# One run of 32 small products or two of 16: where the token sums stand among the dense products of a PEER layer

## The chip, the cores and the metric

One core of a Trainium2 chip runs the whole step as one program. The metric is the device time of one execution in microseconds (us); the time before is the median of three executions. Engines are named as in the profile: PE (matrix products) with its weight loads PEld, DVE, ACT, POOL (GpSimd) and SP, which only issues transfers here.

## The reference

A decoder layer on 576 tokens (512 of a prompt, 64 samples) of width 2048: a modulated norm, a projection, two recurrent branches, an output projection, then a PEER layer and a final norm. The change stands in the PEER layer, cut here to what matters:

```
q   = (h2 @ w_q)                          # 8 heads, two halves of 128
sc  = q . sub_keys                        # 128 first keys, 128 second keys
i1, i2, top = best 16 pairs of each head  # expert = i1 * 128 + i2, 16384 experts
act = gelu(h2 . expert_u[expert]) * softmax(top)
out = sum over heads and picks of act * expert_v[expert]
```

Each token picks 8 x 16 = 128 experts. Expert `(i1, i2)` is one row of 2048 numbers in `u` and one in `v`.

## The kernel before

Experts are kept in 128 blocks, one block for each first key. For the 512 prompt tokens the kernel computes the 80 most picked blocks (`L = 80`) densely, as matrix products over all tokens; picks outside of these, and all picks of the samples, are gathered row by row with indirect DMAs.

**The dense first half (U).** The loop `for n in range(NU2)` has 160 steps, two for each of the 80 blocks. `u_half` does a step: 8 values of `kk`, and at each three products of 128x128 weights with 128x512 numbers (high and low parts of a split, `hhi`, `hlo`, `xhi`, `xlo`), 24 products in all, into one bank `pu`. Even `n` has `k` = 0 to 7, odd `n` has `k` = 8 to 15; then GELU on ACT and a store. The weights of a step come by SP (`raw`), ACT copies out the high part `xhi` and POOL subtracts for the low part `xlo`, two to three steps ahead.

**The token sums.** The dense products need, for each token, how much it weighs each of the experts: a matrix of 128 second keys by 80 blocks. For each token, DVE makes two one-hot matrices of its 128 picks (`op` and `wr`, eight tokens at a time, `g_pair`, L1587), ACT scales one by the softmax (`g_scale`, L1595), and PE multiplies them (`g_mm`, L1601): four products of 32 columns side by side for each token. A block of four tokens fills a bank of PSUM by 16 such products, and ACT copies the bank to a staging tile `stg` (`g_out`, L1608), which is stored to `gd` and read again in the second half. There are 128 blocks, done two at a time: one into the bank `gbank`, one into the bank that `pu` does not use at that time (`other_bank`, tile `gx`). The next block of experts starts in that bank.

**What sets the order.** All engines work their instructions in the order in which the Python code writes them. A planner (`spare`, `upto`, `due_g`) decides in which step a pair of token blocks, a gathered row or a piece of the selection stands. Gathered rows of `u` are fetched by POOL (indirect DMA, `take`, L1234) and multiplied by DVE (L1262).

Of the kernel before, what the change touches and what calls it, by code (L numbers as in the profile page):

```python
# [51 lines left out]
LAG = 3  # L52
# [28 lines left out]
def build(ctx, tc, A, O, dbg=None):  # L81
# [292 lines left out]
    for n in ("lru_wa", "lru_wx"):  # L374
        g = wk.tile([128, KW, 64], F32, name=f"g_{n}")
# [261 lines left out]
    def pbank(tag, nm, bufs):  # L637

        if tag == "u":
            u_turn[0] += 1  # L640
            tag, bufs = f"u{u_turn[0] % 2}", 1
        return psum["p"].tile([128, 512], F32, name=nm, tag=tag, bufs=bufs)

    def other_bank(nm):

        return psum["p"].tile([128, 512], F32, name=nm, tag=f"u{(u_turn[0] + 1) % 2}", bufs=1)
# [196 lines left out]
    def new_row(nm):  # L843
        s_ = free_slot()
        if s_ is None:
            s_ = min(range(slots_now[0]), key=lambda x: held_by[x])
        k = held_by[s_] = len(row_log)
        row_log.append(False)
        return (gp if s_ < RB else pools["vx"]).tile([128, D], F32, name=nm, tag=f"row{s_}", bufs=1), k
# [4 lines left out]
    for i in range(RB):  # L854
        r, k = new_row(f"row0_{i}")
# [75 lines left out]
    def ahead(l, c):  # L931
        while at["l"] <= min(l, len(stream) - 1):
            load(at["l"])
            at["l"] += 1
        while at["c"] <= min(c, len(stream) - 1):
            conv(at["c"])
            at["c"] += 1
# [119 lines left out]
    def sample_twice():  # L1057

        for k0 in range(0, KD, 8):
            r, a = new_row(f"dup{k0}")  # L1060
            row_log[a] = True
            d = r.bitcast(F32R).rearrange("p (q k t) -> p q k t", q=2, t=128)
            dups.append(d)
            for q in range(2):
                S.activation(d[:, q].rearrange("p k (r t) -> p k r t", t=NG),
                             r32(hv[q][:, k0:k0 + 8, None, NA:T]).to_broadcast([128, 8, 2, NG]), AF.Copy)

    def sample_rows():

        hT = first_h["h"] = psum["p"].tile([128, D], F32, name="hT0", tag="hT", bufs=1)  # L1070
        for k in range(KD):
            for q in range(2):
                PE.matmul(hT[:, k * 128:(k + 1) * 128], dups[k // 8][:, q, k % 8, :], identr, start=q == 0, stop=q == 1)
# [310 lines left out]
    def mid(n):  # L1384
        for f in mids.pop(n, ()):
            f()
        if R1 is not None and gk and n % 2 == 0:
            g_eight(n)

    def u_half(n, i, c):  # L1390
        hi, lo = parts.pop(n)
        if c == 0:
            fin["pu"] = pbank("u", f"pu{i}", 2)
        pu = fin["pu"]
        for kk in range(8):
            k = 8 * c + kk
            if kk == 4:
                mid(n)
            for a, (st, mv) in enumerate(((hi, 0), (hi, 1), (lo, 0))):
                PE.matmul(pu, st[:, kk, :], movA[mv](k), start=k == 0 and a == 0, stop=k == KD - 1 and a == 2)  # L1400
        if c == 1:
            act = actp.tile([128, NA], F32, name=f"act{i}", tag="act")
            S.activation(act, pu, AF.Gelu_apprx_tanh)
            if i < L - SG:
                nc.scalar.dma_start(actd[i // SG, :, i % SG, :], act)
            else:
                kept.append(act)
# [161 lines left out]
    gk = {}  # L1569
# [21 lines left out]
    def g_scale(b):  # L1591

        ops, wr, j0 = pair[b]
        for j in range(4):
            S.activation(ops[:, j0 + j, :], ops[:, j0 + j, :], AF.Copy, scale=it[2][:, b * 4 + j:b * 4 + j + 1])  # L1595

    def g_mm(b, pg):
        ops, wr, j0 = pair.pop(b)
        for j in range(4):
            for a in range(0, 128, 32):  # L1600
                PE.matmul(pg[a:a + 32, j * L:(j + 1) * L], ops[:, j0 + j, a:a + 32], wr[:, j0 + j, :],  # L1601
                          start=True, stop=True)

    def g_out(b, pg):
        c, b0 = divmod(b, TC // 4)
        if b0 == 0:
            stg[c] = pools["rg"].tile([128, L, TC], F32, name=f"stg{c}", tag="stg", bufs=2)
        S.activation(stg[c][:, :, b0 * 4:b0 * 4 + 4].rearrange("p i t -> p t i"),  # L1608
                     pg[:, :4 * L].rearrange("p (t i) -> p t i", t=4), AF.Copy)
        if b0 == TC // 4 - 1:  # L1610
            full = stg.pop(c)
            for q in range(0, L, L // 4):
                puts.append(lambda q=q: nc.scalar.dma_start(gd[c][:, q:q + L // 4, :], full[:, q:q + L // 4, :]))

    def put(n):
        for f in puts[:n]:
            f()
        del puts[:n]
# [5 lines left out]
    spare, due_g = -BEHIND, 0.0  # L1624
    R1 = R2 = None
    gm = [0, 0, 0, 0, 0]
    ep = None

    def upto(n):
        return min(NB2, max(0, (n - R1) * NB2 // (E0 - 6 - R1)))  # L1630

    def g_eight(n):

        nonlocal spare
        b = gm[1]
        if b + 2 <= min(upto(n - LAG), gm[2]):
            pgs = gk["g"], other_bank(f"gx{b}")
            for j in range(2):
                g_mm(b + j, pgs[j])
            for j in range(2):  # L1640
                g_out(b + j, pgs[j])
            gm[1] += 2
            spare += 0.8

    for n in range(NU2):
        _, i, c = stream[n]
        if n == 0:
            sample_twice()
        if n == 1:
            sample_rows()  # L1650
        ahead(n + 3, n + 2)
        spare += PIECE if R1 is None else PIECE_G
        scaled = gm[2]
        if R1 is not None:
            put(2)
            if n % 2 and gk:
                g_eight(n)
            if not gk:
                g_start()
            elif gm[0] < min(upto(n), gm[1] + PAIRS - 1):  # L1660
                g_pair(gm[0])
                gm[0] += 2
                spare -= 2.2
            while n > R1 + 5 and gm[2] < min(gm[4], scaled + 4):
                g_scale(gm[2])
                gm[2] += 1
            gm[3:] = gm[0], gm[3]

        even, waits = R2 is not None, False
        while spare > 0 and R2 is None:  # L1670
            cost = next(steps1 if R1 is None else steps2, "end")
            if cost == "end":
                if R1 is None:
                    R1 = n
                else:
                    R2 = n
                break
            if cost is None:
                waits = True
                break  # L1680
            spare -= cost
        if not even:
            if since is None and ready[0]:
                since = n
            if since is not None and n == since + 1:
                fetch_to(RB - 1)
            if R1 is not None and n > R1 + 1 and gf[0] in h_fetch and gf[0] <= gu[0] + 2:
                fetch_to(gf[0] + 1)
            if since is not None and n > since + 2:
                due_g += RATE[R1 is not None] + (0.7 if waits and spare > 4.5 else 0.0)  # L1690
            g0 = gu[0]
            gather_to(due_g, ready[0])
            due_g = min(due_g, gu[0] + 1.0)
            spare -= 2.4 * (gu[0] - g0)
            if waits:
                spare = min(spare, 3.0)
            G0 = gu[0]
        else:
            gather_to(G0 + (NU + EARLY_V - G0) * (n - R2 - (1 - EASE) * max(0, n - E0)) / (EASE * (NU2 - 1) + (1 - EASE) * E0 - R2))
        if n == E0:  # L1700
            assert not pair and not stg
            put(len(puts))
            p2.close()
            epx = ctx.enter_context(ExitStack())
            ep = epx.enter_context(tc.tile_pool(name="ep", bufs=1))
        u_half(n, i, c)
        if n - E0 == 2:
            load_group(0)
        for sg, o in ((0, 1), (1, 7)):
            if 0 <= n - E0 - o < 4:  # L1710
                load_weights(sg, n - E0 - o)
        if n - E0 == 6:
            weigh(0)
        if n - E0 == 7:
            halve(0, 0)
        if n - E0 == 8:
            halve(0, 1)
        if n == NU2 - 2:
            weigh_kept(0)
            weigh_kept(1)  # L1720
        if n == NU2 - 1:
            weigh_kept(2)
# [38 lines left out]
    for i in VO:  # L1761
        c = GT[i][2]
# [3 lines left out]
    for m in range(M):  # L1766
        gi, q, bl, first, final = steps[m]
        n = NU2 + 2 * m
# [12 lines left out]
        for kq in range(KD // VQ):  # L1781
# [9 lines left out]
            k, pv = v_column(n, gi, q, bl, first, final, kq)  # L1791
# [34 lines left out]
    with tc.If(any_ > 0), tc.tile_pool(name="fb", bufs=1) as fp:  # L1826
        io1 = fp.tile([128, 128], F32, name="f_io1")
        V.tensor_scalar(io1, iota, 1.0, None, op0=ALU.add)
        for i, (p0, n, c) in enumerate(GT):
# [8 lines left out]
            kk = pick_keys(R_, f"f{i}", fp, io1, kb)  # L1838
# [117 lines left out]
```

## Time and profile before

| | |
|---|---|
| median of 3 executions | 3203.68 us (3203.2 to 3206.89) |
| the profiled execution | 3219.74 us, its span 3217.9 us |
| PE busy, share of the span | 3038.3 us, 94% |
| PE share of the chain that ended last | 74% |
| granted TensorE clock, mean | 0.978 |
| stretch of the token sums, from the span's start | 1526.7 to 2121 us |

PE's time in the profile is modelled and its products overlap: a 128x512 product is shown with some 390 ns, yet products start some 230 ns apart. So what PE costs is read from the starts of its instructions, not from their durations. In the profile each of the small products stands as two (the 16 of a token block as x32), since they multiply plain fp32 numbers. "Issue" as a reason for idle time means that the profile shows nothing that the engine waited for.

### The profile page before, as it was taken

To read this page: it belongs to the slowest core of one execution; us is meant where nothing else is said; L and a number is where in the kernel's file an instruction comes from. 1 tells how busy PE (TensorE), PEld (TensorE's weight loads), DVE (VectorE), ACT (ScalarE), POOL (GpSimd) and SP (SyncE) were. 2 spreads that over 40 slices of the span, in tenths; PEclk is the share of its full clock that TensorE was granted. 3 is DMA by queue.
4 is the path that set the end of the run, shared out by engine and by line. 5 is a ranking of instruction groups with operands and counts; after the bars stand their busy time and mean duration, and the time that the engine had idled before them with its cause. 6 is when DMAs were issued, how large, how long until landed. Compare 5 with 4: busy or idle time off the path is not lost.

```text
span 3217.9 us, 52757 instructions
## 1 busy us (share of the span) xinstructions
PE 3038.3 (94%) x20313; PEld 2568.9 (80%) x20313; DVE 2242.0 (70%) x3296; ACT 1042.8 (32%) x1645; POOL 1793.7 (56%) x1093
## 2 busy tenths in 40 slices
PE   5899999999989999999999999998999999889897
PEld 2688798899979898887887777787878778677776
DVE  5355521234356797988999988867787898888955
ACT  3244311123232223232655555532322222122222
POOL 2233233344333335666666666667877788777842
PEclk8999999999989999999999999999999999999998
DMA  9834465633332226999879998999999997999963
GB/s 364 308 132 139 159 215 203 213 111 117 130 134 101 73 74 216 314 326 373 339 300 378 365 398 324 371 389 362 367 403 401 400 358 286 372 372 371 352 207 138
DMA packets 257650, 881.13 MB, mean 274 GB/s; under 512 B 37190, under 2 KB 38086, under 8 KB 203494
## 3 DMA queue, kind: packets, MB, share of 16 engines
q0 software_dynamic: 75472, 454.32, 36.1%
q1 hardware_dynamic: 161760, 382.48, 33.7%
q10 hardware_dynamic: 20160, 40.90, 3.3%
q8 instruction: 160, 2.62, 0.3%
q14 instruction: 98, 0.80, 0.1%
HBM read 878.84 MB, written 65.76 MB: 294 GB/s over the span
## 4 chain that ended last, share of the span: by engine, by line
PE 74%; DMA 11%; DVE 7%; issue 4%; POOL 2%; ACT 1%; SPq 0%; POOLq 0%; ACTq 0%; DVEq 0%
PE pu L1400 25%; PE pv L1423 15%; PE pp_o L139 6%; DMA v<-v,rows 5%; PE pp_s L139 3%; PE pp_c L139 3%; PE pp_x L139 3%; PE pp_b L139 3%; PE qb L139 3%; PE pp_y L139 2%; PE qa L139 2%; PE ada L189 2%; DMA wa<-w_ada 2%; DMA raw<-vq 2%; DVE accB L1290 2%
## 5 line engine op out<-in xcount | busy, mean ns | idle before, releaser
L926 POOL TENSOR_TENSOR xlo<-raw,xhi 128x1024 fp32r<-128x1024 f32 x320 | 783.5, 2460 | 365.6 <-ACT xhi L925 359.4
L1262 DVE SCALAR_TENSOR_TENSOR u<-u,hT 128x2048 f32<-128x2048 f32 x223 | 504.8, 2283 | 126.9 <-DMA u<-u,rows 124.9
L1290 DVE SCALAR_TENSOR_TENSOR accB<-v,dots,accB 128x2048 f32<-128x2048 f32 x211 | 496.5, 2353 | 133.5 <-DMA v<-v,rows 128.8
L925 ACT ACTIVATE xhi<-raw 128x1024 fp32r<-128x1024 f32 x320 | 338.4, 1062 | 749.3 <-PE pv L1423 251.8
L1423 PE MATMUL pv<-ahi,xhi 128*128 128x512 f32 x1280 | 509.3, 398 | 49.6 <-DVE acc L1445 40.7
L1400 PE MATMUL pu<-hhi,xhi 128*128 128x512 f32 x1280 | 507.1, 396 | 1.0 <-ACT qt L949 0.7
L1423 PE MATMUL pv<-alo,xhi 128*128 128x512 f32 x1280 | 505.3, 395 | 2.3 <-DVE alo L1374 2.3
L1423 PE MATMUL pv<-ahi,xlo 128*128 128x512 f32 x1280 | 504.5, 394 | 1.2 <-POOL xlo L926 1.2
L1400 PE MATMUL pu<-hhi,xlo 128*128 128x512 f32 x1280 | 498.6, 390 | 2.3 <-POOL xlo L926 2.3
L1400 PE MATMUL pu<-hlo,xhi 128*128 128x512 f32 x1280 | 498.9, 390 | 0.0
L1423 PEld LDWEIGHTS pv<-ahi,xhi 128*128 128x128 f32 x1280 | 244.5, 191 | 109.4 <-DVE acc L1445 27.6
L1234 POOL DMA_INDIRECT v<-v,rows x223 | 265.7, 1191 | 78.9 <-issue 40.6
L1234 POOL DMA_INDIRECT u<-u,rows x223 | 225.1, 1009 | 116.1 <-DVE u L1262 68.0
L1400 PEld LDWEIGHTS pu<-hhi,xhi 128*128 128x128 f32 x1280 | 240.3, 188 | 58.8 <-issue 1.7
L1423 PEld LDWEIGHTS pv<-ahi,xlo 128*128 128x128 f32 x1280 | 244.4, 191 | 53.5 <-POOL xlo L926 1.6
L1423 PEld LDWEIGHTS pv<-alo,xhi 128*128 128x128 f32 x1280 | 244.7, 191 | 52.6 <-DVE alo L1374 2.6
L1400 PEld LDWEIGHTS pu<-hhi,xlo 128*128 128x128 f32 x1280 | 240.4, 188 | 54.3 <-POOL xlo L926 3.6
L1400 PEld LDWEIGHTS pu<-hlo,xhi 128*128 128x128 f32 x1280 | 240.6, 188 | 47.4
L1595 ACT ACTIVATE op<-op,it 128x128 f32<-128x128 f32 x512 | 155.9, 389 | 1.2 <-issue 0.8
L128 POOL TENSOR_TENSOR wlo_q<-raw_q,whi_q 128x1024 fp32r<-128x1024 f32 x28 | 68.2, 2438 | 149.0 <-ACT whi_q L126 145.8
L189 PE MATMUL ada<-wa,cpad 128*32 128x512 f32 x768 | 106.5, 650 | 43.2 <-DMA wa<-w_ada 43.0
L128 POOL TENSOR_TENSOR wlo_o<-raw_o,whi_o 128x1024 fp32r<-128x1024 f32 x32 | 77.6, 2426 | 115.9 <-ACT whi_o L126 115.9
(505 smaller groups left out, 5655.9 us busy)
## 6 DMA issues: line engine op xcount, KB each, us to landing
wa<-w_ada SPq DMA_DIRECT2D x96, 1024.0 KB
raw<-ut SPq DMA_DIRECT2D x160, 512.0 KB
raw<-vq SPq DMA_DIRECT2D x320, 256.0 KB
gd<-stg ACTq DMA_DIRECT2D x64, 320.0 KB
gsb<-gd POOLq DMA_DIRECT2D x80, 256.0 KB
actd<-act ACTq DMA_DIRECT2D x76, 256.0 KB
actr<-actd POOLq DMA_DIRECT2D x19, 1024.0 KB
raw_o<-w_out SPq DMA_DIRECT2D x32, 512.0 KB
```

Of the source, the lines that this page charges most:

```text
L128: lo_engine(share).tensor_sub(lo, raw, r32(hi))
L139: PE.matmul(o, st, mv[pick](k), start=first, stop=last)
L189: PE.matmul(acc[32 * g:32 * g + 32, :], cpad[:, 4 * kq + g, :], w[:, g, :], start=kq == 0, stop=kq == 3)
L925: S.activation(hi, raw, AF.Copy)
L926: G.tensor_sub(lo, raw, r32(hi))
L1234: G.indirect_dma_start(out=out, out_offset=None, in_=src, in_offset=bass.IndirectOffsetOnAxis(ap=idx, axis=0), bounds_check=NE * 128 - 1, ...
L1262: V.scalar_tensor_tensor(r, r, 1.0, st["h"], op0=ALU.mult, op1=ALU.mult, accum_out=dots[i][:, j:j + 1])
L1290: V.scalar_tensor_tensor(st["a"], r, dots[i][:, j:j + 1], st["a"], op0=ALU.mult, op1=ALU.add)
L1400: PE.matmul(pu, st[:, kk, :], movA[mv](k), start=k == 0 and a == 0, stop=k == KD - 1 and a == 2)
L1423: PE.matmul(pv, st, mv, start=first and j == 0 and a == 0, stop=last and not end and j == SG - 1 and a == 2)
L1595: S.activation(ops[:, j0 + j, :], ops[:, j0 + j, :], AF.Copy, scale=it[2][:, b * 4 + j:b * 4 + j + 1])
```

## The change

`g_eight` did the two token blocks of a pair one right behind the other: 32 small products without a dense one between, then the two copies on ACT. It stood ahead of a step's dense products for odd `n`, and ahead of `kk` = 4 for even `n`. `g_four` does the first block at `k` = 3 (even `n`) or 9 (odd `n`) and the second at `k` = 6 or 12, so that nine dense products (three values of `k`) stand between the two blocks. Which step a pair falls into is set by the same planner.

```
@@ mid
-        if R1 is not None and gk and n % 2 == 0:
-            g_eight(n)
@@ u_half, for each kk
+            if R1 is not None and gk:
+                g_four(n, 8 * c + kk)
@@ build
-    def g_eight(n):
+    second = []
+
+    def g_four(n, k):
         nonlocal spare
-        b = gm[1]
-        if b + 2 <= min(upto(n - LAG), gm[2]):
-            pgs = gk["g"], other_bank(f"gx{b}")
-            for j in range(2):
-                g_mm(b + j, pgs[j])
-            for j in range(2):
-                g_out(b + j, pgs[j])
-            gm[1] += 2
-            spare += 0.8
+        if k in (3, 9):
+            b = gm[1]
+            if b + 2 <= min(upto(n - LAG), gm[2] if k == 3 else scaled):
+                g_mm(b, gk["g"])
+                g_out(b, gk["g"])
+                second.append(b + 1)
+                gm[1] += 2
+                spare += 0.8
+        elif k in (6, 12) and second:
+            bank = other_bank(f"gx{second[0]}")
+            g_mm(second[0], bank)
+            g_out(second.pop(), bank)
@@ the loop over n, ahead of g_start and g_pair
-            if n % 2 and gk:
-                g_eight(n)
```

On PE, at an even step (block 28 of the experts): `pu` is the bank of the dense products, `wr` and `op` are the one-hot matrices of the tokens. Before:

```order
L1400 MATMUL pu_14282<-hhi,xlo_14079 128x512
L1601 MATMUL gbank<-wr_13982,op_13981 32x80 x16
L1601 MATMUL gx_14295<-wr_13982,op_13981 32x80 x16
L1400 MATMUL pu_14282<-hhi,xhi_14078 128x512
L1400 MATMUL pu_14282<-hlo,xhi_14078 128x512
L1400 MATMUL pu_14282<-hhi,xlo_14079 128x512
```

On PE, the same step of the changed kernel:

```order
L1601 MATMUL gbank<-wr_13982,op_13981 32x80 x16
L1400 MATMUL pu_14282<-hhi,xhi_14078 128x512
L1400 MATMUL pu_14282<-hlo,xhi_14078 128x512
L1400 MATMUL pu_14282<-hhi,xlo_14079 128x512
...
L1601 MATMUL gx_14318<-wr_13982,op_13981 32x80 x16
L1400 MATMUL pu_14282<-hhi,xhi_14078 128x512
```

The two runs, which stood together, now have nine dense products between them; the same products are done, and PE has as many instructions as before.

On ACT, at the odd step that follows (`xhi` is the high part of weights for a later step, `op` the scaling of one-hot matrices, `stg` the copies of the two banks, `act` the GELU). Before:

```order
L925 ACTIVATE xhi_14347<-raw_14258 128x1024
L1608 ACTIVATE stg_14158<-gbank 128x4x80
L1608 ACTIVATE stg_14158<-gx_14351 128x4x80
L1595 ACTIVATE op_14217<-op_14217,it_13229 128x128 x8
L1403 ACTIVATE act_14430<-pu_14282 128x512
```

On ACT, the same step of the changed kernel:

```order
L925 ACTIVATE xhi_14347<-raw_14258 128x1024
L1595 ACTIVATE op_14182<-op_14182,it_13229 128x128 x8
L1608 ACTIVATE stg_14138<-gbank 128x4x80
L1608 ACTIVATE stg_14138<-gx_14400 128x4x80
L1403 ACTIVATE act_14430<-pu_14282 128x512
```

In odd steps the copies of the banks now stand behind the scaling; in even steps ACT's order is as before. On DVE, at two places, one-hot pairs and a few row products change places with instructions of the selection of picks; on POOL and SP the order is the same.

## The prediction

> **What bounds the kernel now.** I read the page first, then the stretch of the token sums by windows, its chain, and single runs in order of time.
>
> ```profile
> span 3217.9 us, 52757 instructions
> PE 3038.3 (94%) x20313; PEld 2568.9 (80%) x20313; DVE 2242.0 (70%) x3296; ACT 1042.8 (32%) x1645; POOL 1793.7 (56%) x1093
> ```
>
> 94% is a share over stages with different limits; the change touches one of them. The windows of that stretch (columns: length, busy time and count of PE, PEld, DVE, ACT, POOL, then granted clock, DMA share, GB/s), and its chain:
>
> ```profile
> 1520.00:1700.00 180.00, 178.77 (x1898) 143.66 (x1900) 164.64 (x268) 108.81 (x243) 113.53 (x75) 1.00 0.83 319
> 1700.00:1900.00 200.00, 195.80 (x2042) 157.47 (x2032) 181.17 (x261) 114.69 (x252) 122.03 (x81) 1.00 0.98 383
> 1900.00:2123.00 223.00, 219.23 (x2332) 176.02 (x2332) 185.13 (x202) 130.42 (x282) 142.63 (x96) 1.00 0.93 365
> ...
> by line: PE pu L1400 83.5%; PE gbank L1601 7.5%; PE gx L1601 7.4%; issue 1.7%; POOL u L1234 0.0%; POOLq L1234 0.0%
> ```
>
> The chain is PE all the way, at the full clock. DMA at 0.98 and DVE at 181 of 200 us are close behind, yet the only wait that PE shows is one without a releaser:
>
> ```profile
> PE gx L1601 <- issue: 9.0, 22, 0.5
> ```
>
> So here every us that PE spends more or less is a us of the span. Two things decide: what a run of small products costs PE besides the products, and what these 22 waits are. A run with no wait, PE alone (start, duration, instruction, count):
>
> ```profile
> 1711.30 0.39 PE L1400 MATMUL pu<-hlo,xhi 128*128 128x512 f32 x1
> 1711.53 0.39 PE L1400 MATMUL pu<-hhi,xlo 128*128 128x512 f32 x1
> 1711.85 0.76 PE L1601 MATMUL gbank<-wr,op 128*32 128x80 f32 x32
> 1712.43 0.74 PE L1601 MATMUL gx<-wr,op 128*32 128x80 f32 x32
> 1713.09 0.50 PE L1400 MATMUL pu<-hhi,xhi 128*128 128x512 f32 x1
> 1713.43 0.40 PE L1400 MATMUL pu<-hlo,xhi 128*128 128x512 f32 x1
> 1713.67 0.39 PE L1400 MATMUL pu<-hhi,xlo 128*128 128x512 f32 x1
> ```
>
> The step between dense products comes from a long row of them:
>
> ```profile
> 1499.98 26.75 PE pu L1400 x118
> ```
>
> 26.75 / 118 = 0.2267 us. A half (one token block) takes 1712.43 - 1711.85 = 0.58. From the last dense product ahead to the third behind are 2.14 us in place of three steps, 0.68: the run costs 1.46, of which two halves are 1.16. The other 0.30 is the way in and out: the first small product starts 0.32 after the dense one (0.09 over a step), the way out takes 0.66 after `gx` begins (0.08 over a half), the second dense product comes after 0.34 (0.11 over), the third after 0.24 (0.01 over).
>
> A run with waits, PE and POOL:
>
> ```profile
> 1687.84 1.00 POOL L1234 DMA_INDIRECT u<-u,rows  x1
> 1688.10 0.39 PE L1400 MATMUL pu<-hhi,xlo 128*128 128x512 f32 x1
> 1688.42 0.76 PE L1601 MATMUL gbank<-wr,op 128*32 128x80 f32 x32
> 1688.99 0.44 PE L1601 MATMUL gx<-wr,op 128*32 128x80 f32 x11
> 1689.14 1.00 POOL L1234 DMA_INDIRECT u<-u,rows  x1 [0.31 <-issue]
> 1689.88 0.34 PE L1601 MATMUL gx<-wr,op 128*32 128x80 f32 x4 [0.44 <-issue]
> 1690.62 0.53 PE L1601 MATMUL gx<-wr,op 128*32 128x80 f32 x17 [0.40 <-issue]
> 1691.08 0.50 PE L1400 MATMUL pu<-hhi,xhi 128*128 128x512 f32 x1
> ```
>
> From dense to dense it took 2.98 us, against 1.56 (1711.53 to 1713.09) without waits. The first 43 small products run at full pace, then two gaps come, while POOL issues indirect DMAs. All of them, summed over the stretch (busy PE and PEld of the dense products, with counts; then the first run of all, which started slowly):
>
> ```profile
> 1526.40:2121.10 594.70, 500.79 (x2127) 394.00 (x2126) 1.00 0.91 357
> ...
> 1526.73 1.01 PE gbank L1601 x32
> 1527.74 1.17 PE gx L1601 x32
> ```
>
> 2127 x 0.2267 = 482.2; 64 pairs x 1.46 = 93.4; 594.7 - 575.6 = 19.1 are left, of which the first run's slow start is 0.43 + 0.5 (1.01 against 0.58, 1.17 against 0.66). So about 18.2 us of PE time are such gaps, in this profiled execution.
>
> **The change part by part.** *Removed:* nothing of the work; the 128 blocks, their copies and the dense products stay. *Added:* a second way in and out for each of 64 pairs: 64 x 0.30 = 19.2 us, all on PE, so on the chain. It could cost as little as 0 (if a way were paid by the pair) and 64 x 0.34 = 21.8 with the 0.34 of the second dense product as the roughest single row; I take 19.2, since the row splits it into delays at each edge. [...]
>
> *The gaps.* A half alone hardly has them. Here an indirect DMA is issued over the whole first half:
>
> ```profile
> 2063.38 1.00 POOL L1234 DMA_INDIRECT u<-u,rows  x1 [0.64 <-DVE u L1262]
> 2063.40 0.76 PE L1601 MATMUL gbank<-wr,op 128*32 128x80 f32 x32
> 2063.97 0.45 PE L1601 MATMUL gx<-wr,op 128*32 128x80 f32 x14
> 2064.71 0.59 PE L1601 MATMUL gx<-wr,op 128*32 128x80 f32 x18 [0.28 <-issue]
> ```
>
> The first half takes 0.57, as without one; the gap comes after 32 + 14. And dense products right behind a run, under an indirect DMA, keep their pace (0.33, 0.24):
>
> ```profile
> 2092.98 1.00 POOL L1234 DMA_INDIRECT u<-u,rows  x1 [0.72 <-PE gbank L1601]
> 2093.29 0.50 PE L1400 MATMUL pu<-hhi,xhi 128*128 128x512 f32 x1
> 2093.62 0.40 PE L1400 MATMUL pu<-hlo,xhi 128*128 128x512 f32 x1
> 2093.86 0.39 PE L1400 MATMUL pu<-hhi,xlo 128*128 128x512 f32 x1
> ```
>
> So PE has some 40 small products in hand, and a run of 32 rows with 2 us of dense products behind it should leave at most 0.5 us of gaps in all. In a profiled execution the gaps' 18.2 go, nearly as much as the ways cost: 3219.74 + 19.2 - 18.2 + 0.5 = 3221.2, a span of about 3219.
>
> *The timed executions* are what counts, and the trace doesn't show them. The profiled one took 3219.74, the median is 3203.68: 16.06 less. The gaps can be in the timed executions too (18.2 to gain), or be what the profiler adds (0 to gain). PE's gaps come at its fastest burst, some 128 instructions with their loads in 1.16 us, and nothing in the program is waited for there. I take the whole 16.06 for them, which leaves 18.2 - 16.06 = 2.1 us of gaps in the timed executions. Sum: 19.2 - 2.1 + 0.5 = +17.6, so 3203.68 + 17.6 = 3221.
>
> *ACT* does the same work. In odd steps the copies move behind the scaling:
>
> ```profile
> L1608 ACT ACTIVATE stg<-gx x64: 777/822/850, 1531.3 to 2122.1; 128x320 f32<-128x320 f32 x64
> L1595 ACT ACTIVATE op<-op,it x512: 351/389/409, 1526.1 to 2117.0; 128x128 f32<-128x128 f32 x171
> ```
>
> The second bank must be copied before the next block of experts starts in it. The run at `k` = 12 ends 12 steps and two runs after the odd step began, 2.7 + 1.8 = 4.5 us; ACT has by then done `xhi` and 8 x 0.39 = 3.1 us of scaling, then copies for some 0.8 + 0.8. That is 6.1, and the step lasts 5.4 + 1.8 = 7.2: hidden by 1.1 us. If it were late, the first dense product of a new block would wait. *DVE, POOL, SP:* the order is the same but for two places on DVE, which nothing on PE waits for; nothing.
>
> *Behind the stretch* the dense half `v` follows on PE; what PE waits for there on POOL and ACT is little:
>
> ```profile
> PE pv L1423 <- ACT xhi L925: 6.8, 3, 3.8
> ```
>
> A slower first half gives the gathered rows time to catch up; that may return 0 to 6.8 us. I take 0, as rows are issued in the order of the steps.
>
> **The rivals.** *The gaps are real in every execution* (no change, chance 0.32): then 19.2 - 18.2 + 0.5 = +1.5, 3205. For it: they go with POOL's indirect DMAs, work of the program. Against it: the profiled execution is longer by nearly their sum. It decides from 12.8 us of real gaps, which leave less than 6.4 (0.2%, about what a measurement of this kernel can tell from no change). [...]
>
> *The gaps are real, and the way out is cheaper after a half* (faster, 0.11): the 0.11 at the second dense product may be a weight load that came late because PE's store of instructions was empty after 64. With a half it would not be: 128 x 0.11 = 14.1 less, 3205 - 14 = 3191. From 0.062 a way on it is faster by over 0.2%. Against it: the 0.34 stands behind runs without gaps as behind those with them.
>
> *The gaps are real and stay* (slower, 0.07): the runs now stand where other indirect DMAs are issued. With as much as now, 3203.68 + 19.2 = 3223; with as much for each half as now for a pair, 18.2 more, 3241.
>
> **How the numbers follow.** The forecast (0.50): 3221, by itself 3212 (6.8 given back, some 2 us of gaps more) to 3226 (2.6 more for the ways, the 2.1 not gained). Slower by over 0.2%: 0.50 + 0.07 = 0.57; within: 0.32; faster: 0.11. The range must take in 3205: 3202 to 3226 leaves out the faster rival and the upper part of the last one, under 2 in 10.
>
> **What the profile of the changed kernel would show.** 128 runs of 32 rows, each 0.32 + 0.67 = 0.99 from dense to dense; PE's wait `gx <- issue` from 9.0 to under 1; the stretch of the sums within 3 us of its length, the span near 3219, and the timed median nearly as long as the profiled execution. If the median stays near 3205 beside such a profile, my reading of the 16.06 is wrong; if runs take less than 0.9, that of the ways.

## The result: 3223 us beside 3204, and 3224 to 3225 beside 3216 to 3217 on other chips

The changed kernel took 3222.96 us (median of 5, 3218.19 to 3223.77) beside 3203.68 (5, 3202.07 to 3206.89): 19.3 us more, a ratio of 1.0055 [1.0041, 1.0070]. That is 2 us over the forecast. Two of the later jobs (each job ran on a chip of its own) gave 1.0022 [1.0014, 1.0031] and 1.0024 [1.0014, 1.0034], because the kernel *before* took 3216 to 3217 there. The first number came out, then, but one of the reasons given for it didn't hold; most of the runs below are about that.

The page of the changed kernel (its profiled execution took 3222.28 us):

```profile
span 3220.5 us, 52736 instructions
...
PE 3052.5 (95%) x20313; PEld 2557.7 (79%) x20313; DVE 2232.5 (69%) x3296; ACT 1053.8 (33%) x1645; POOL 1793.2 (56%) x1093
```

Its stretch of the token sums, by windows (columns as before):

```profile
1520.00:1700.00 180.00, 179.54 (x1865) 138.12 (x1867) 163.16 (x266) 111.34 (x240) 110.23 (x73) 1.00 0.82 316
1700.00:1900.00 200.00, 200.00 (x2059) 154.90 (x2048) 180.47 (x261) 119.95 (x254) 122.95 (x81) 1.00 0.97 383
1900.00:2123.00 223.00, 223.00 (x2301) 172.40 (x2300) 181.35 (x201) 133.67 (x281) 140.04 (x94) 1.00 0.91 359
```

PE now shows 200.00 of 200 us, where it had 195.80, and does about as many instructions (2059, before 2042). It has lost its idle time and gained as much work that isn't products. All that PE waits for in this stretch (columns: us in total, times, longest):

```profile
PE gbank L1601 <- ACT op L1595: 0.5, 1, 0.5
```

The 22 waits `gx <- issue` are gone, and ACT's copies, moved behind the scaling, stop PE nowhere. A half run, PE and POOL in order of time:

```profile
1647.92 0.39 PE L1400 MATMUL pu<-hhi,xlo 128*128 128x512 f32 x1
1648.12 1.00 POOL L1234 DMA_INDIRECT u<-u,rows  x1 [0.16 <-DVE u L1262]
1648.23 0.76 PE L1601 MATMUL gx<-wr,op 128*32 128x80 f32 x32
1648.93 0.50 PE L1400 MATMUL pu<-hhi,xhi 128*128 128x512 f32 x1
1649.26 0.40 PE L1400 MATMUL pu<-hlo,xhi 128*128 128x512 f32 x1
1649.42 1.00 POOL L1234 DMA_INDIRECT u<-u,rows  x1 [0.30 <-DVE op L1587]
1649.50 0.39 PE L1400 MATMUL pu<-hhi,xlo 128*128 128x512 f32 x1
```

From the dense product ahead to the third behind it takes 1649.50 - 1647.92 = 1.58, less three steps (0.68) 0.90 us; an indirect DMA lies over it and makes no gap. In the trace 127 of the 128 halves cost 0.90. The stretch, from the first small product to the last, with the dense products of U alone:

```profile
1523.10:2125.00 601.90, 521.97 (x2139) 391.71 (x2139) 1.00 0.90 354
```

It is 7.2 us longer than in the trace of before (594.70), with 12 more dense products in it (2139, before 2127: 2.7 us). Nothing tells on which chip that trace of before was taken.

In what follows, the *cost* of a run is the start of the third dense product behind it minus the start of the last one ahead, less three steps of 0.2267 us. A *gap* is more than 0.12 us between the starts of two neighbouring small products, and counts with what it has over the 0.0172 us that a row takes on average. Both are summed over a whole trace. Rows of small products are counted as the profile shows them, 32 to a token block. The first run of every trace starts slowly: in the kernel before it has 5 or 6 gaps, some 0.8 to 1.0 us, with or without indirect DMAs. A run is *under an issue* when an instruction of POOL that issues an indirect DMA overlaps the time that the run takes without gaps (1.16 us for 64 rows); the first run is left out of these counts.

### The profile page after: what moved, and what is told of

It reads as the page before. It is cut to its first block, busy times and chain, and to the rows that moved or that the text cites. A ratio compares the mean times of both kernels' runs of the same rounds, so it can differ in the third digit from the quotient of the medians.

```text
span 3220.5 us, 52736 instructions
## 1 busy us (share of the span) xinstructions
PE 3052.5 (95%) x20313; PEld 2557.7 (79%) x20313; DVE 2232.5 (69%) x3296; ACT 1053.8 (33%) x1645; POOL 1793.2 (56%) x1093
## 4 chain that ended last, share of the span: by engine, by line
PE 71%; DMA 14%; DVE 6%; issue 4%; POOL 3%; ACT 1%; SPq 0%; POOLq 0%; DVEq 0%; ACTq 0%
PE pu L1400 24%; PE pv L1423 12%; PE pp_o L139 6%; DMA raw<-vq 5%; DMA v<-v,rows 4%; PE pp_s L139 3%; PE pp_c L139 3%; PE pp_x L139 3%; PE qb L139 3%; PE pp_b L139 3%; PE pp_y L139 2%; PE ada L189 2%; PE qa L139 2%; DMA wa<-w_ada 2%; POOL xlo L926 1%
## 5 line engine op out<-in xcount | busy, mean ns | idle before, releaser
L1400 PE MATMUL pu<-hhi,xhi 128*128 128x512 f32 x1280 | 514.7, 402 | 1.2 <-ACT qt L949 0.7
```

## First job: undo, place, split finer, pay one way more

Two theories stood against each other. By the forecast's, the profiler adds PE's gaps, and timed executions hardly have them. By the rival's, they belong to every execution. Four kernels, on one chip.

**The kernel before, unchanged** (no edit).

> The kernel before, not changed. Theory (the gaps inside the runs of small products belong to the profiled execution): timed 3203 to 3206; the profiled execution some 16 us longer than the timed ones, with about 18 us of gaps in the stretch of the token sums. Rival (the gaps are in every execution, and the 16 us between the profiled and the timed executions of before have another cause): timed the same, the profiled execution longer or not, but its gaps don't account for it.

Measured: 3215.84 us (11 executions, 3213.78 to 3226.02), ratio 1.0002 [0.9993, 1.0011]; the kernel before had 3217.52 in this job. The profiled execution took 3214.67, among the shortest. PE's waits in the stretch:

```profile
PE gx L1601 <- issue: 9.1, 24, 0.5
```

The gaps are there (33, 15.8 us in all), and the profiled execution is as long as the others. So on this chip the gaps are in all executions, and the profiler doesn't add them. 30 of the 63 runs are under an issue, and 17 of these have gaps; of the other 33 none has (in the trace of before: 14 of 30, and none of 33). None of these runs, in either trace, has a gap before 42 of its rows have started. The whole job was 14 us slower than the 3203.68 of the first comparison, nearly the sum of the gaps.

**Long runs in the middle of a step** (`k` = 4 or 12).

```
@@ u_half, for each kk (both old calls of g_eight removed)
+            if R1 is not None and gk and 8 * c + kk in (4, 12):
+                g_eight(n, gm[2] if c == 0 else scaled)
```

> Pairs of token blocks stay together, 64 runs of 64 rows, but all at k = 4 and k = 12, in the middle of a step, where before no run had a gap. Theory: the profiled execution loses its gaps (PE's wait gx <- issue under 2 us, span about 3202), and the timed one stays at 3204 (3200 to 3208), so that the two are as long. Rival (gaps real in every execution): the timed one falls by the gaps' 18 us to about 3186. Rival (the cost of the change lies in where the runs stand, not in their number): slower, towards 3213 to 3223.

Measured: 3212.84 us, ratio 0.9988 [0.9979, 0.9997]. PE's waits in the stretch:

```profile
PE pu L1400 <- ACT stg L1608: 3.9, 7, 1.7
PE gx L1601 <- issue: 2.7, 7, 0.4
```

64 long runs with 16 gaps (5.9 us) in place of 33 (15.8): the gaps go with the place of the run, not with its length alone. Only 23 runs are under an issue now, 7 of them with gaps. Neither the theory's time (3200 to 3208) nor the rival's (3186) came out, and `k` = 4 was not free of gaps before: in the trace of before 10 of 32 runs at the head of an odd step and 4 of 31 at `k` = 4 have some. The time fell by 4.7 us (from 3217.52), not by the 9.9 of the gaps. 3.9 us stand there as a new wait: in the odd steps the copies were late, and the dense products of the next block had no bank. Where the run stands earlier (`k` = 3 and 11, below), that wait is gone.

**Quarters**: two tokens at a time, at `k` = 3, 4, 6, 7 and 9, 10, 12, 13.

```
-    def g_mm(b, pg):
+    def g_mm(b, pg, js=range(4)):
...
+        elif k in (4, 10) and second:
+            g_mm(second[0] - 1, gk["g"], range(2, 4))
```

> The changed kernel with each token block split once more: 256 runs of 8 small products (16 rows), three dense products between the two of a block and six or three to the next block. Theory (0.30 to 0.36 us for each way out of the dense products and back): 128 ways more than the changed kernel, 128 x 0.30 to 0.36 = 38 to 46 us, so 3261 to 3269. Rival (the cost of the change is the wait for banks and copies or the place, not the way): about the changed kernel, 3223.

Measured: 3268.69 us, ratio 1.0158 [1.0144, 1.0172]. A quarter, PE in order of time:

```profile
1698.18 0.40 PE L1400 MATMUL pu<-hhi,xlo 128*128 128x512 f32 x1
1698.51 0.48 PE L1601 MATMUL gx<-wr,op 128*32 128x80 f32 x16
1698.92 0.50 PE L1400 MATMUL pu<-hhi,xhi 128*128 128x512 f32 x1
1699.26 0.39 PE L1400 MATMUL pu<-hlo,xhi 128*128 128x512 f32 x1
1699.49 0.40 PE L1400 MATMUL pu<-hhi,xlo 128*128 128x512 f32 x1
```

1699.49 - 1698.18 - 0.68 = 0.63 us. With 0.90 for a half that gives 16 rows in 0.27, and a way of 0.63 - 0.27 = 0.36. All 256 quarters cost 161.9 us, 45.5 more than the 128 halves (116.4), for 128 ways more: 0.355 each. The timed difference to the changed kernel's 3223 (timed on other chips) is 45. The kernel is 51 us slower than before on its own chip.

**A lone product**: before, with one small product more, by itself among dense ones, four values of `k` after a pair.

```
+            if k in (7, 11) and lone:
+                lone.clear()
+                PE.matmul(gk["g"][0:32, 432:512], ident[:, 0:32], iota[:, 0:80], start=True, stop=True)
```

> The kernel before, pairs together at their old places, and one extra product of 32 columns by 80 on constants into unused columns of gbank, nine dense products behind each pair: work that the reference doesn't need, and nothing waits for it. Theory (a way out and in costs 0.30 whatever is done there): 64 x (0.30 + some 0.04 for the product, which stands as two) = 22 us, 3222 to 3228. Rival (the cost of the change hangs on the second block's bank, copies or length of run): 3204 to 3207.

Measured: 3244.97 us, ratio 1.0090 [1.0077, 1.0104]: 27.5 us for 64 of them, 0.43 each (from the trace 0.46).

```profile
1708.46 0.39 PE L1403 MATMUL pu<-hhi,xlo 128*128 128x512 f32 x1
1708.78 0.33 PE L1401 MATMUL gbank<-iota,ident 128*32 128x80 f32 x2
1709.04 0.50 PE L1403 MATMUL pu<-hhi,xhi 128*128 128x512 f32 x1
1709.38 0.39 PE L1403 MATMUL pu<-hlo,xhi 128*128 128x512 f32 x1
1709.61 0.39 PE L1403 MATMUL pu<-hhi,xlo 128*128 128x512 f32 x1
```

A single product of 32 columns, two rows in the profile, costs as much time as two dense ones (0.4534), nearly all of it the way in and out: 0.46 less two rows (0.03) are 0.43, more than a longer run pays (0.35), and more than the 0.34 a piece that the theory had. The long runs kept their gaps (31, 15.9 us) here. A way is paid by the run, down to the 2 rows of this one.

## Second job: without the indirect DMAs

What makes the gaps? While the prompt's token sums are computed, POOL issues 160 of the 223 indirect DMAs of rows of `u`. I took these out, in the kernel before and in the changed one.

```
+        quiet[0] = R1 is not None and bool(gk) and n < E0
...
+            if not quiet[0]:
+                take(held[j][0], A["u"], rows_i[i][:, j:j + 1])
```

**The changed kernel again** (no edit to it).

> The changed kernel again, beside the kernel before on one chip. Theory, mended by e1 to e4 (the gaps inside the long runs, 18.8 us in the stretch, are in these timed executions, and two ways in and out cost 2 x 0.90 - 1.455 = 0.355 a pair, 22.7 us): the two nearly cancel, the changed kernel is 3 to 9 us slower than before (1.001 to 1.003). Rival (as recorded: the timed executions have no such gaps): 17 to 23 us slower, as on the first chip (1.0055).

Measured: 3223.5 us beside 3216.42 (24 executions, 3211.52 to 3222.85), ratio 1.0022 [1.0014, 1.0031], 7.1 us slower, as this theory had it. In its trace 54 halves are under an issue, and none of them has a gap.

**Before, without these rows.**

> The kernel before without 160 of its 223 indirect DMAs of u rows, those that POOL issues between the first of the token sums and step 146; DVE does its products on the old rows, by zero, so the gathered part is left out there. Theory (gaps come while POOL issues indirect DMAs, and are in the timed executions): PE's wait gx <- issue is gone in the profile and the time falls by 15 to 25 us against before. Rival (gaps come from the run's length alone): the wait stays at 9 us. Rival (gaps not in timed executions): the wait goes, and the time stays within 5 us.

Measured: 3193.59 us, ratio 0.9921 [0.9908, 0.9934]. PE waits for nothing in the stretch (no row is left), 62 of 64 long runs cost 1.45 us, and the gaps fall to 1.0 us.

**Changed, without these rows.**

> The changed kernel without the same 160 indirect DMAs. Theory: no gaps to win here, so it is slower than e6_norow_before by the ways alone, 0.355 x 64 = 20 to 25 us. Rival (part of the cost of two runs comes from POOL's indirect DMAs in them): less than 15 us.

Measured: 3213.0 us, ratio 0.9985 [0.9976, 0.9993], 19.4 us slower than the kernel above, just under the 20 to 25. The runs of this kernel cost 116.4 us, as with the rows.

Without the rows the kernel before is 22.8 us faster and the changed one 10.5. If the 10.5 is what fewer rows save in either kernel, the other 12.3 are the gaps. In the traces they are 14.5 (15.5 and 1.0), and the cost of the long runs falls by more, from 111.9 to 94.0 us, since in the runs under an issue other rows come late too, by less than a gap: in the trace of before 10 of the 16 such runs without a gap cost 1.50 to 1.54, and all 33 runs under no issue 1.455. So the gaps need the indirect DMAs. This edit takes out the issues and the transfers alike. The counts of the first job speak for the issues: no run apart from one has a gap there, though the DMA engines are busy throughout (0.92 of the stretch). And with no gaps in either kernel, the split costs 3213.0 - 3193.59 = 19.4 us, as much as the 19.3 of the first comparison. That points to a kernel before without gaps there.

**Long runs at `k` = 3 and 11**, the edit of the middle run with other numbers, one place earlier.

> Pairs together, 64 runs, all at k = 3 and k = 11, one value of k earlier than in e2_mid, so that ACT's copies are ahead of the next block of experts. Theory: the waits of 5 us for ACT that e2_mid showed are gone and few gaps come, so 8 to 14 us faster than before. Rival (gaps follow the runs, since POOL's indirect DMAs stand where PE's runs do): as before.

Measured: 3207.93 us, ratio 0.9972 [0.9961, 0.9984], 15.6 us less than the changed kernel. 56 of 64 runs are clean (1.45 us): only 12 are under an issue, and 6 of these have gaps. The copies are in time:

```profile
PE gx L1601 <- issue: 2.2, 6, 0.4
PE gbank L1601 <- ACT op L1595: 1.2, 1, 1.2
```

## Third and fourth job: fewer ways, and the kernel before once more

**Three blocks in a run**: if a way costs 0.35 us, fewer and longer runs should pay, as far as the gaps let them. A block's four tokens use 320 columns of a bank; here six tokens (480) go into one, so three blocks fit in two banks. The places are those of the run before.

```
@@ g_eight
+        m = min(3, NB2 - b)
+            for t in range(4 * m):
+                ops, wr, j0 = pair[b + t // 4]
+                o = t % 6 * L
...
+                    PE.matmul(pgs[t // 6][a:a + 32, o:o + L], ...)
```

> As e8_early (runs at k = 3 and k = 11), but three token blocks a run: six tokens (480 columns) in each of the two banks, 43 runs in place of 64, 96 rows each (the last 64). Theory (0.354 us for each way, 0.0172 a row): 21 ways fewer, 7.4 us less than e8_early, if no more gaps come; with 96 rows a run is twice as far beyond the 43 that PE has in hand, so some 3 to 6 us of gaps more: 3202 to 3207 beside a before of 3216, that is 0.996 to 0.998. Rival (the length of a run decides, and POOL's indirect DMAs hit every long one): gaps of 10 us more than in e8_early, and no gain on it.

Measured: 3199.31 us (11) beside 3203.37 (21 executions, 3198.48 to 3210.08), ratio 0.9981 [0.9972, 0.9990]. 36 of 43 runs cost 2.01 us; one of them:

```profile
1925.16 0.39 PE L1400 MATMUL pu<-hhi,xlo 128*128 128x512 f32 x1
1925.48 1.04 PE L1643 MATMUL gbank<-wr,op 128*32 128x80 f32 x48
1926.33 1.01 PE L1643 MATMUL gx<-wr,op 128*32 128x80 f32 x48
1927.28 0.50 PE L1400 MATMUL pu<-hhi,xhi 128*128 128x512 f32 x1
1927.61 0.40 PE L1400 MATMUL pu<-hlo,xhi 128*128 128x512 f32 x1
1927.85 0.39 PE L1400 MATMUL pu<-hhi,xlo 128*128 128x512 f32 x1
```

(1927.85 - 1925.16 - 0.68 = 2.01.)

All runs together cost 88.5 us, against 94.2 in the next kernel, and the time is 4.1 us less than before. The theory's 3202 to 3207 was meant for a chip with gaps; this one has none, as the next run shows, so its rival is not tested here.

**The kernel before, in the same job.**

> The kernel before, not changed, to see whether its time and its gaps are those of e1 in another job. If the gaps are absent, the time is 3200 to 3205, as on the first chip, and the wait gx <- issue is under 2 us; if they are there, 3212 to 3220 with a wait of 9 us. A time of 3203 with the wait at 9 us would say that the profiled execution differs from the timed ones.

Measured: 3203.46 us (11, 3199.72 to 3211.3), ratio 0.9998 [0.9989, 1.0007]. This chip is the one that has no gaps but those of the first run (6, 1.0 us; 62 of 64 long runs cost 1.45). It is not that PE's runs and POOL's issues miss each other: 33 of the 63 runs are under an issue, and none has a gap. The 19th run of the trace, under two issues, PE and POOL:

```profile
1689.13 0.99 POOL L1234 DMA_INDIRECT u<-u,rows  x1
1689.39 0.39 PE L1400 MATMUL pu<-hhi,xlo 128*128 128x512 f32 x1
1689.71 0.76 PE L1601 MATMUL gbank<-wr,op 128*32 128x80 f32 x32
1690.28 0.74 PE L1601 MATMUL gx<-wr,op 128*32 128x80 f32 x32
1690.45 1.00 POOL L1234 DMA_INDIRECT u<-u,rows  x1 [0.33 <-DVE u L1262]
1690.95 0.50 PE L1400 MATMUL pu<-hhi,xhi 128*128 128x512 f32 x1
```

The same run of the same kernel on the first job's chip, with the same two issues at nearly the same places (0.58 us ahead of the run and 0.72 behind its start; above 0.58 and 0.74):

```profile
1687.20 0.99 POOL L1234 DMA_INDIRECT u<-u,rows  x1
1687.46 0.39 PE L1400 MATMUL pu<-hhi,xlo 128*128 128x512 f32 x1
1687.78 0.76 PE L1601 MATMUL gbank<-wr,op 128*32 128x80 f32 x32
1688.36 0.49 PE L1601 MATMUL gx<-wr,op 128*32 128x80 f32 x12
1688.50 1.00 POOL L1234 DMA_INDIRECT u<-u,rows  x1 [0.30 <-issue]
1689.24 0.36 PE L1601 MATMUL gx<-wr,op 128*32 128x80 f32 x4 [0.39 <-issue]
1689.99 0.52 PE L1601 MATMUL gx<-wr,op 128*32 128x80 f32 x16 [0.39 <-issue]
1690.44 0.50 PE L1400 MATMUL pu<-hhi,xhi 128*128 128x512 f32 x1
```

In the one, 64 rows run through from 1689.71 to 1690.95. In the other the same 64 take from 1687.78 to 1690.44, 1.42 us longer. The stretch, dense products of U alone, of this kernel and then of the same one in the first job:

```profile
1528.90:2104.95 576.05, 499.99 (x2125) 393.77 (x2124) 1.00 0.92 364
```

```profile
1526.30:2120.50 594.20, 500.72 (x2126) 394.33 (x2127) 1.00 0.92 358
```

18.2 us, with the same products: the gaps' whole worth in this stretch, from one chip to another. The whole executions differ by less, 12.4 us between the medians (3215.84 and 3203.46), close to the 12.3 of the second job. Some of the rest is given back in what follows, the last dense products of U up to its end, of this trace and then of the first job's, each with all of PE's waits there:

```profile
2104.95:2209.60 104.65, 98.17 (x408) 79.01 (x408) 0.95 0.93 357
...
PE pu L1400 <- POOL xlo L926: 4.9, 4, 1.8
PE pu L1400 <- ACT xhi L925: 1.4, 1, 1.4
```

```profile
2119.80:2214.20 94.40, 93.45 (x408) 76.19 (x408) 1.00 0.93 355
...
PE pu L1400 <- POOL xlo L926: 0.8, 2, 0.6
```

Without gaps PE waits 6.3 us there for the parts of the weights, with them 0.8. The granted clock differs too (0.95 and 1.00), and these are single traces. The profiled executions, 3211.3 and 3214.67 us, are only 3.4 apart, since this one is the longest of its 11.

**Three blocks, on a further chip.**

> e9_three again, in another job. Theory (whether gaps come differs from job to job with the chip; a way costs 0.354 us): where before takes 3203 (no gaps), 3196 to 3200, ratio 0.997 to 0.999; where before takes 3216 (gaps), runs of 96 rows at k = 3 and k = 11 have some gaps of their own, 3200 to 3210, ratio 0.995 to 0.998. Rival (the gain of e9 hangs on the chip): no gain on before with gaps.

Measured: 3202.52 us (5) beside 3217.49 (15), ratio 0.9954 [0.9941, 0.9968]. This chip has gaps, and the 43 runs show them: 24, 8.2 us, 1.7 of these in the first run, with 8 of the 15 runs under an issue stopped. That is fewer than 64 runs have at the old places.

**The changed kernel, there.**

> The changed kernel once more in the same job. Theory: its time doesn't depend on the gaps, 3220 to 3226 in either case: 1.005 to 1.007 of a before that takes 3203, 1.001 to 1.003 of one that takes 3216. Rival (the two ratios measured so far are scatter of one value): about 1.004 in either case.

Measured: 3225.32 us (11), ratio 1.0024 [1.0014, 1.0034]; its runs cost 116.4 us, and PE's waits `gx <- issue` are absent. So the changed kernel takes 3223 to 3225 us in all three comparisons, and the interval leaves out the rival's 1.004.

All jobs in one table (us):

| | before | changed | difference | gaps in traces of before |
|---|---|---|---|---|
| first comparison | 3203.68 | 3222.96 | +19.3 | not traced there |
| first job | 3217.52 | - | - | 15.8 |
| second | 3216.42 | 3223.5 | +7.1 | not traced there |
| second, no rows | 3193.59 | 3213.0 | +19.4 | 1.0 |
| third | 3203.37 | - | - | 1.0 |
| fourth | 3217.49 | 3225.32 | +7.8 | not traced there |

The changed kernel was not run in the third job, so that +19 belongs to a chip without gaps is shown only by the second job's kernels without rows.

## Why the prediction was right, and where it wasn't

- **The ways: right in kind, 3 us too small.** Each kernel here fits 0.354 us for a way in and out and 0.0172 for each row: 16, 32, 64, 96 rows in 0.63, 0.90, 1.455, 2.01. Splitting costs 2 x 0.902 - 1.455 = 0.35 a pair, or 22.3 for the 64 pairs in place of 19.2. The failed step is "two halves are 1.16": the start of `gx` 0.58 after that of `gbank` was taken for what a half takes. By the fit, 32 rows take 0.55, so two halves are 1.10, and 0.35 of the run's 1.455 are left for the way, not 0.30. Comparing two runs of different length (0.902 and 1.455) would have shown it. The runs show 0.35 us a way from 16 to 96 rows, and 0.43 around the lone product's 2; none shows what PE does in that time.
- **A half has no gaps: right.** 3 gaps and 0.5 us, all in the first run of the trace, though 57 of its halves are under an issue. The two later traces of the changed kernel have 54 and 52 such halves, without a gap, on chips where long runs have them. A half ends at row 32, and behind the first run no gap came before row 42. That PE has some 40 small products in hand was the author's estimate from such rows; no run shows what it holds.
- **ACT: right.** The moved copies made no wait in the profiled execution; 1.4 to 1.7 us in two others.
- **The 16.06 us between profiled execution and median: the reason was wrong, and the forecast's 3221 came out by luck.** The step "I take the whole 16.06 for them", with the profiler as cause, gave the right number for that comparison, since the kernel before most likely ran there without the gaps that its trace shows. But the profiling doesn't add the gaps: with gaps, the profiled execution is no longer than the others of its job (3214.67 among 3213.78 to 3226.02), and in the third job, where it was the longest (3211.3 beside a median of 3203.46), it had none. Traces and times were taken to be of the same chip in the same condition; the shown trace fits the 3217 of jobs with gaps, the shown times the 3203 of the job without. No trace of the kernel before in the first comparison is there to prove it. The sign named for a wrong reading, a median near 3205, could not come there, where the kernel before was itself timed without gaps.
- **The rival "the gaps are real in every execution" fits three of four later chips.** Its +1.5 came out as +7.1 and +7.8 on the two where the changed kernel ran: 3.1 more for the ways, and 5.9 less gained, if the gaps are worth 12.3 in the timed executions and not 18.2; some 3 of this came back, as below. The 12.3 is no measurement beside the +7.1, since both come from the same four times (19.4 - 7.1); the 12.4 between the medians of two chips is one.
- **"The way out is cheaper after a half" is refuted:** the second dense product comes as late behind a half (0.33: 1649.26 - 1648.93), a quarter (0.34: 1699.26 - 1698.92) and a lone product (0.34: 1709.38 - 1709.04) as behind a pair (0.34), so it doesn't hang on how many rows stand ahead. An empty store of instructions was the author's guess, and no run shows one.
- **The signs named ahead:** 1.01 from dense to dense (said 0.99), `gx <- issue` gone, span 3220.5 (said 3219), median 0.7 us above the profiled execution: right. The stretch grew by 7.2, not "within 3": some 1.5 were in the sum, 3.1 are the ways', and 2.7 the dense products' that now fall inside it.
- **Given back: not in the sum.** Against the kernel before without gaps (576.05) the stretch grew by 25.9. Its 14 more dense products are 3.2 of that, and 22.7 are left, about the ways' 22.3. The time grew by 19.3 only, so some 3 us come back outside the stretch. The prediction had 0 to 6.8 there and took 0. In the traces PE waits behind the stretch, up to the end of U, 6.3 us for POOL's `xlo` and ACT's `xhi` in that kernel before and 3.2 (2.7 and 0.5) in the changed one: 3.1 less, which is what is missing. The granted clock there differs as well (0.95 and 0.98), and it is one trace each, so this is a likely place and not a settled one.

What stays open is why PE stops while an indirect DMA is issued on some chips and not on another. The kernels are the same and so is the granted clock in the stretch (1.00); the runs lie under issues as often (30 of 63, and 33 without a gap). Each chip was seen in one job only, so what belongs to the chip and what to the job can't be told apart.

## What to carry to other kernels

A run of 32-column products among full ones cost some 0.35 us here for getting in and out, with 16 to 96 rows, and 0.43 with 2. Make such runs few and long, and place them where no bank is waited for and where POOL issues no indirect DMA: 43 runs of three blocks at `k` = 3 and 11 beat the kernel before, 0.9981 [0.9972, 0.9990] on the chip without gaps and 0.9954 [0.9941, 0.9968] on one with them, where they beat the changed kernel too. And before a difference between a trace and a median is given a cause, run the same kernel again on several chips: here the unchanged kernel differs by 12 to 14 us between one chip's job and another's, most of the 16.06.

## What the runs showed of the hardware that wasn't expected

- One kernel took 3203 us on one chip and 3216 to 3217 on three others, in medians of 15 to 24 executions, at the same clock in the stretch in the two traces there are (1.00): where it took longer, PE's bursts of small products stopped while POOL issued indirect DMAs (15.8 us of gaps in a trace of one of the three, against 1.0 on the fast chip, all of it in the first run). Of the 63 runs behind the first, 30 and 33 were under an issue; 17 of the 30 stopped, and none of the 33.
- Such a burst went at least 42 rows far before the first gap, at the old places mostly 43 to 46. In the run shown PE then got 4 rows in 0.75 us (1689.24 to 1689.99) while the DMA was issued and just after. Runs of 32 rows kept their pace under an issue: none of 106 halves on two chips with gaps was stopped.
- A single small product, 32 columns of weights and 80 moving ones, cost PE 0.46 us among dense ones: as much as two dense products of 128 and 512.
